# A hybrid attention and convolution layer: the low parts of the first phase's weights made on VectorE, some operands made anew, and the convolution paced by stretch

## The chip, the cores and the metric

One core of a Trainium2 chip. Its engines are TensorE (PE, with its weight loads as PEld), VectorE (DVE), ScalarE (ACT), GpSimd (POOL) and SyncE (SP, which here only issues DMAs). The metric is device time in microseconds (us) of one execution, the median of several runs. Six views of one profiled execution are used: the page, busy time by windows, groups of instructions by line, waits, one line's instructions, and the timeline.

## The reference

One layer over x of 2048 rows by 1024 channels, float32. x is normalised by row, then multiplied by `w_in` (1024 x 9216), whose columns fall into nine parts of 1024: q, k, v, a gate z for the attention, a value and a gate for the convolution, a gate z for the convolution, and two merge gates.

```python
h = x @ w_in
q, k, v, z_sb, c_val, c_gate, z_cv, g_sb, g_cv = jnp.split(h, SPLIT_POINTS, axis=-1)
o_sb = _stick_breaking_attention(to_heads(q), to_heads(k), to_heads(v)).reshape(bsz, seq, SB_WIDTH)
y_sb = (o_sb * jax.nn.silu(z_sb)) @ w_sb_proj
u = c_val * jax.nn.sigmoid(c_gate)
u = _causal_depthwise_conv(u, conv_w, conv_b)
u = jax.nn.silu(_layer_norm(u, conv_ln_g, conv_ln_b))
y_cv = (u * jax.nn.silu(z_cv)) @ w_cv_proj
merged = jax.nn.sigmoid(g_sb) * y_sb + jax.nn.sigmoid(g_cv) * y_cv
return _layer_norm(DEEPNORM_ALPHA * x + merged @ w_out, ln_g, ln_b)
```

The attention has 16 heads of 64; a weight is a sigmoid of a logit times the product of (1 - sigmoid) of the keys between. The convolution has 31 taps for each channel and is causal.

## The kernel before, in words

Every large product is made of float32r operands in two parts: a high part (a value rounded to float32r by a copy on ACT) and a low part (the value minus its high part). A product is then three matmuls: high by high, high by low, low by high. The helper `split` (L115 to L117) makes both parts, with ACT for the high and DVE for the low.

The sequence is held in four chunks of 512 rows, chunks 3 and 2 being half 1 and chunks 1 and 0 half 0. There are three stages.

**First phase** (`first_phase`, L741). It makes part of `x @ w_in` in *groups*. A group takes two blocks of 128 columns and both chunks of a half, and splits the 1024 inputs into two: a product of 2 x 2 blocks. Winograd's form of Strassen's scheme needs seven block products for it (P1 to P7) instead of eight. Each is 12 matmuls of 128 x 512 (`prod`, L906: four blocks of 128 inputs, three matmuls each), so a group is 84, in 14 pieces of six. Half 1 has 36 groups: eight u (value and gate of the convolution) and 28 of k, q, v, z, c, g and h (m = 0 to 3; g and h are the two merge gates). Half 0 has 20: eight u and twelve of c, g and h. Its k, q, v and z are made later, by the plain scheme, in the attention stage.

A group's seven weight operands come from four raw blocks: `raws` (L861) loads them, 256 KB each, on SP's queue, one group ahead. `w_op` (L869) makes one operand: for four of the seven a sum or difference on DVE first (`diff`, L877), then the high part on ACT (L891), then `low` (L901). `low` writes the negated high part into the low part's place (ACT, L902), and an accumulating DMA issued by POOL adds the raw block to it (L903). Raw blocks and differences go round in eight buffers (`raw_tile`), the operands in nine (`op_tile`). A finished operand of 512 KB is stored to device memory by SP's queue (L895, issued at L93): for k, q, v and z three of the seven, which the later stages load again; for u, c, g and h all seven, which half 0 loads instead of making them (`kept`, L873).

In a group, the seven results share PSUM banks: after P7, DVE adds its bank into the tile `gt` (L961, recorded at L757), and P4, which is issued after the next group's P1, goes on accumulating into that same bank. So P4 can't start before that addition has read it. The operands of x are made from rows that are normalised and transposed (L788, L818), and swapped for the other half's at the end of half 1 (`swap`).

**Attention stage.** The attention of half 1, then of half 0, woven with the rest of `x @ w_in`, the convolution's norm and the projections. **Output stage**: the last projections and the output product.

The convolution runs on DVE as a background job through the first two stages. A generator (`conv_steps`) makes one instruction a step: 51 steps for 128 channels and a half, 46 of them taps (L409), and two empty ones where its input wasn't loaded ahead. `slow_step` (L1115) is called after each piece of matmuls: it adds a pace to a counter and runs one step when the counter is at least 1. The pace is `PACES[phase]`: 1.0 in the first phase, 0.6 after. The counter is cut to 1 only in calls that run no step.

Order: TensorE's order is written out by hand; the other engines' instructions are put in an order by a scheduler when the kernel is built, by priority (`use` functions get 500 places of precedence, convolution steps go 800 back and at least 3 pieces late). On the chip each engine and each DMA queue runs in that order and waits at its head.

Of the kernel before, what the change touches and what calls it, by code (L numbers as in the profile page):

```python
# [8 lines left out]
F32 = mybir.dt.float32  # L9
F32R = mybir.dt.float32r  # L10
AF = mybir.ActivationFunctionType
ALU = mybir.AluOpType
# [15 lines left out]
NBW = 4  # L28
LEAD = 4.0
LAG = 3  # L30
PACES = [1.0, 0.6]
I0 = 1
SPLIT = 0.27
RD = 9
# [20 lines left out]
def layer_kernel(ctx: ExitStack, tc, x, w_in, w_sb, w_cv, w_out, vecs, cw, rows, out):  # L55
# [7 lines left out]
    nc = tc.nc  # L63
# [27 lines left out]
    def dma(dst, src):  # L91

        nc.sync.dma_start(out=dst.bitcast(F32) if dst.dtype == F32R else dst,  # L93
                          in_=src.bitcast(F32) if src.dtype == F32R else src)
# [42 lines left out]
    def st(dt=F32):  # L137
        return sg_p.tile([P, CH], dt, name="st", tag="st", bufs=7)
# [20 lines left out]
    class Fill:  # L159
# [7 lines left out]
        def add(self, cost, fn):  # L167
            self.pieces.append((cost, fn))
            for e in self.later:
                e[0] -= 1  # L170
            due = [e[1] for e in self.later if e[0] <= 0]
            self.later = [e for e in self.later if e[0] > 0]
            self.pieces += due
# [69 lines left out]
    def half(h):  # L243
        return (2 * h + 1, 2 * h)
# [32 lines left out]
    def use_qk(dr, i):  # L277
        def use(c, ps):
            hi, lo = st(F32R), st(F32R)
            split(ps, hi, lo)  # L280
            dma(dr[c, i][0], hi)
            dma(dr[c, i][1], lo)
        return use

    def v_parts(i):
        vs = {}

        def use(c, ps):
            v, vs[c] = st(), st()
            nc.scalar.activation(v, ps, AF.Copy)  # L290
            dma(vtd[c, i], v)
            n = CH - 1
            nc.vector.tensor_tensor(out=vs[c][:, :n], in0=v[:, 1:], in1=v[:, :n], op=ALU.subtract)
            if c == NCH - 1:
                nc.gpsimd.tensor_scalar(out=vs[c][:, n:], in0=v[:, n:], scalar1=-1.0, scalar2=None, op0=ALU.mult)
            else:
                nc.gpsimd.tensor_tensor(out=vs[c][:, n:], in0=vnext[:, i:i + 1], in1=v[:, n:], op=ALU.subtract)
            if c:
                nc.gpsimd.tensor_copy(out=vnext[:, i:i + 1], in_=v[:, 0:1])

        def turn(c):
            tp = tpt()
            for j in range(4):
                nc.tensor.transpose(out=tp[:, j * P:(j + 1) * P], in_=vs[c][:, j * P:(j + 1) * P], identity=ident)
            for a in range(2):
                t = st(F32R)
                tv = t.rearrange("p (b e d) -> p b e d", b=4, e=2)
                split(tp.rearrange("p (b e d) -> p b e d", b=4, e=2)[:, :, a], tv[:, :, a], tv[:, :, 1 - a])
                dma(vdr[c, i, a], tv.rearrange("p b e d -> p b (e d)"))

        return use, lambda F, c: F.delay(3, 0.44, lambda: turn(c))
# [24 lines left out]
    def gated(m, h):  # L336

        val, gate = {}, {}

        def put(c):  # L340
            if c not in val or c not in gate:
                return
            u = st()
            nc.vector.tensor_tensor(out=even_odd(u), in0=val.pop(c), in1=gate.pop(c), op=ALU.mult)
            q = c % 2 * 256
            dma(udr[h, m][:, :, q:q + 256], u.rearrange("p (e n) -> p e n", e=2))
            if c == 2 * h:
                slow.append(conv(m, h))

        def use_v(c, ps):  # L350
            val[c] = ps
            put(c)

        def use_g(c, ps):
            nc.scalar.activation(ps, ps, AF.Sigmoid)
            gate[c] = ps
            put(c)

        return use_v, use_g
# [381 lines left out]
    def first_phase(F, x2, w1, ps_p):  # L741
# [8 lines left out]
        def x_op(op, f):  # L750
            pool, tag = (x2, op) if op in ("S2", "S3", "S4") else (xa, "SX" if op == "S1" else op)
            t = [pool.tile([P, CH], F32R, name=tag + e) for e in "hl"]
            xo.setdefault(op, []).append(t)
            split(f, *t)
# [85 lines left out]
        def swap(op):  # L840

            def one(k):
                if k == 0:
                    xo[op] = []
                f = st()
                dma(f, {"A11": fdr[1][:, k], "A12": fdr[1][:, k + 4], "A22": fdr[0][:, k + 4]}[op] if op[0] == "A" else sdr[op, k])
                x_op(op, f)
            return [(0, lambda k=k: one(k)) for k in range(4)]
# [50 lines left out]
                    wdr[id(w_in), g["cols"][p == P3], int(p != P1)] = d  # L899

        def low(t, src):  # L901
            nc.scalar.activation(t[:, 1], t[:, 0].bitcast(F32), AF.Copy, scale=-1.0)  # L902
            nc.gpsimd.dma_start(out=t[:, 1], in_=src.bitcast(F32R), accum_op=ALU.add)  # L903


        def prod(g, p, part, bank, start=False):  # L906
# [68 lines left out]
        kept = {}  # L975

        def group(h, e, m):
            g = {"h": h, "after": [None, None]}
            if e == "u":
                g["cols"] = COL_CV + m * P, COL_CG + m * P  # L980
                g["uses"] = gated(m, h)
            else:
                i = 2 * m, 2 * m + 1
                base = {"k": COL_K, "q": COL_Q, "v": COL_V}.get(e) if e in "kqv" else blocks[e][0]
                g["cols"] = tuple(base + n * P for n in i)
                if e == "v":
                    g["uses"], g["after"] = zip(*(v_parts(n) for n in i))
                elif e in "kq":
                    g["uses"] = [use_qk(kdr if e == "k" else qdr, n) for n in i]
                else:  # L990
                    g["uses"] = [(silu_to if e in "zc" else sig_to)(n, blocks[e][1]) for n in i]
            if h == 0:
                g["kept"] = kept[e, m]
            else:
                g["keep"] = "some" if e in "kqvz" else "all"
                g["to"] = kept.setdefault((e, m), {})
            return g

        def order(h):
# [21 lines left out]
        for n, g in enumerate(groups):  # L1021
            nxt = groups[n + 1] if n + 1 < len(groups) else None
            last = nxt is None or nxt["h"] != g["h"]
            first = n == 0
            pc = pieces(g, nxt)
            if nxt and not first:
                F.add(0, lambda nxt=nxt: raws(nxt))

            def emit(p, extra=()):
                extra = list(extra)  # L1030
                for q in pc[p]:
                    F.add(*q)
                    if extra:
                        F.extend([extra.pop(0)])
                F.extend(extra)
                if first and p < 3:
                    for q in (4 + p,):
                        F.add(0, lambda q=q: w_op(groups[0], q))
                if last and p != P4 and nxt is not None:
                    F.extend(swap(XOP[p]))  # L1040

            emit(P1, two[:2] if first else ())
            if prev is not None:
                for q in prev[P4]:
                    F.add(*q)
                if prev_g["after"][0]:
                    prev_g["after"][0](F, half(prev_g["h"])[1])
                if prev_g["h"] != g["h"]:
                    F.extend(swap("A22"))

            def w_start():
                for p in (0, 1, 2):
                    w_next(p)

            def w_next(p):
                if nxt:
                    F.add(0, lambda nxt=nxt: w_op(nxt, p))

            if not first:
                w_start()  # L1060
            emit(P2, two[2:] if first else ())
            if g["after"][0]:
                g["after"][0](F, c1_of(g))
            if not first:
                w_next(3)
            emit(P5)
            if first:
                F.add(0, lambda nxt=nxt: raws(nxt))
                w_start()
                w_next(3)  # L1070
            w_next(4)
            emit(P6)
            w_next(5)
            emit(P3)
            if g["after"][1]:
                g["after"][1](F, c1_of(g))
            w_next(6)
            emit(P7)
            if g["after"][1]:
                g["after"][1](F, half(g["h"])[1])  # L1080
            prev, prev_g = pc, g
# [17 lines left out]
    def c1_of(g):  # L1099
        return half(g["h"])[0]  # L1100
# [3 lines left out]
    F = Fill()  # L1104
# [4 lines left out]
    phase = [0]  # L1109
# [5 lines left out]
    def slow_step(now=False):  # L1115
        marks.append(newest())
        pace[0] += PACES[phase[0]]
        if not now and (not slow or pace[0] < 1):
# [22 lines left out]
        emit_fill(len(F.pieces))  # L1141
    F = Fill()
    n_done[0] = 0
    phase[0] = 1


    with ExitStack() as s2:
# [169 lines left out]
```

## Time and profile before

| what | us |
| --- | --- |
| median of 3 runs (3349.89 to 3355.69) | 3353.22 |
| the profiled execution | 3352.82 |
| its span, first to last instruction | 3351.0 |
| TensorE matmuls busy | 2948.6 (88%) |
| VectorE busy | 2423.2 (72%) |
| ScalarE busy | 1540.5 (46%) |
| GpSimd busy | 291.8 (9%) |

Busy time counts the time in which at least one instruction of the engine runs. A window row gives, for a stretch of the span, the busy time of each engine with its number of instructions, the mean clock granted to TensorE (1.00 is full), the mean busy share of the 16 DMA engines and their GB/s. A row of groups gives a line, engine, operation, output and inputs by the program's names, shapes and count; then the busy time and the mean of one in ns; then the idle time of the engine just before, and what ended it. A row of waits gives who waited for whom, the total in us, how often, and the longest. SPq is the sequencer of SP, which issues DMAs. Matmuls overlap in their records: the distance of two starts is what one costs.

### The profile page before, as it was taken

Reading aid. Unit: us, or ns where it says so; the run is one execution under the profiler, and the core shown is the slowest. Engines: PE = TensorE matmul, PEld = TensorE weight load, DVE = VectorE, ACT = ScalarE, POOL = GpSimd, SP = SyncE. Lnnn points to the kernel's source line nnn. Section 1 sums busy time; section 2 is a strip of 40 time slices with the busy share of each in tenths; the row PEclk is TensorE's granted clock in tenths of the full one; section 3 lists DMA queues with packets and bytes.
Section 4 is the critical chain, followed back from the end, with each engine's and each line's share of the span. In section 5 each row is a group of like instructions: output and inputs, shape, how many; then the busy total and the mean of one; then the engine's idle time right before and its main releaser. Section 6 shows DMA issues by size and latency. Waiting matters only on the chain.

```text
span 3351.0 us, 42860 instructions
## 1 busy us (share of the span) xinstructions
PE 2948.6 (88%) x14666; PEld 2433.7 (73%) x14666; DVE 2423.2 (72%) x3219; ACT 1540.5 (46%) x2792; POOL 291.8 (9%) x414
## 2 busy tenths in 40 slices
PE   6676788878888999989998998999899989889998
PEld 4555666767677888778877777778778777667887
DVE  6542676554654866689899889898897888966746
ACT  7554454545453212245555455555564555543322
POOL 2222222222220000000000000000000000000000
PEclk9888888989899999999999999999999999989999
DMA  7999999999999877675656344354543544478462
GB/s 203 275 274 300 281 286 302 272 287 292 286 284 326 262 247 255 226 220 184 192 189 190 117 153 156 120 172 140 162 143 125 159 156 137 151 238 275 140 203 82
DMA packets 364203, 708.86 MB, mean 212 GB/s; under 512 B 42448, under 2 KB 84560, under 8 KB 363856
## 3 DMA queue, kind: packets, MB, share of 16 engines
q1 hardware_dynamic: 327696, 640.05, 57.3%
q0 software_dynamic: 36288, 66.08, 11.4%
q8 instruction: 115, 1.88, 0.2%
q14 instruction: 104, 0.85, 0.1%
HBM read 371.47 MB, written 268.44 MB: 191 GB/s over the span
## 4 chain that ended last, share of the span: by engine, by line
PE 36%; DVE 17%; issue 11%; DMA 6%; ACT 3%; SPq 1%; POOL 1%; DVEq 0%; POOLq 0%; ACTq 0%
PE mm L201 10%; DVE nb L589 8%; PE pb L910 6%; PE pp L910 4%; PE mm L910 4%; PE pv L628 4%; DVE tl L117 4%; PE tp L612 4%; PE lg L583 2%; PE lg L584 2%; SPq L93 1%; ACT nb L586 1%; ACT th L116 1%; DMA st<-ydq 1%; PE mo L1242 1%
## 5 line engine op out<-in xcount | busy, mean ns | idle before, releaser
L116 ACT ACTIVATE th<-tp 128x512 fp32r<-128x512 f32 (+1 forms) x576 | 330.1, 574 | 447.8 <-PE tp L612 437.1
L117 DVE TENSOR_TENSOR tl<-tp,th 128x512 fp32r<-128x512 f32 (+1 forms) x576 | 372.9, 650 | 89.8 <-ACT th L116 87.2
L612 PE MATMUL tp<-ident,nb 128*128 128x128 f32 x2176 | 352.7, 278 | 74.1 <-DVE nb L589 58.5
L586 ACT ACTIVATE nb<-lg 128x512 f32<-128x512 f32 (+3 forms) x640 | 331.1, 532 | 115.7 <-PE lg L584 113.5
L589 DVE TENSOR_TENSOR_SCAN nb<-nb,dd 128x256 f32<-128x256 f32 (+7 forms) x256 | 343.3, 1346 | 16.1 <-ACT nb L586 16.1
L628 PE MATMUL pv<-tl,v 128*128 128x256 f32 (+1 forms) x1152 | 303.2, 292 | 43.4 <-DVE tl L117 42.5
L612 PEld LDWEIGHTS tp<-ident,nb 128*128 128x128 f32 x2176 | 255.1, 142 | 108.9 <-DVE nb L589 72.0
L589 DVE TENSOR_TENSOR_SCAN nb<-nb,zero 128x1024 f32<-128x1024 f32 x128 | 299.8, 2345 | 22.3 <-ACT nb L586 22.0
L628 PE MATMUL pv<-th,v 128*128 128x256 f32 (+1 forms) x1152 | 307.8, 285 | 2.4 <-ACT th L116 2.2
L583 PE MATMUL lg<-k,qd 128*128 128x512 f32 (+3 forms) x640 | 267.6, 419 | 22.3 <-ACT nb L586 10.7
L628 PEld LDWEIGHTS pv<-tl,v 128*128 128x128 f32 x1152 | 219.0, 190 | 81.7 <-DVE tl L117 66.4
L584 PE MATMUL lg<-k,ql 128*128 128x512 f32 (+3 forms) x640 | 234.4, 366 | 0.0
L628 PEld LDWEIGHTS pv<-th,v 128*128 128x128 f32 x1152 | 219.3, 190 | 20.5 <-ACT th L116 4.6
L409 DVE SCALAR_TENSOR_TENSOR cy<-cu,csum,cy 128x512 f32<-128x512 f32 x240 | 179.3, 747 | 25.4 <-ACT cy L405 20.2
L201 PE MATMUL mm<-A11h,w 128*128 128x512 f32 x512 | 184.4, 406 | 11.6 <-ACT w L116 6.1
L201 PE MATMUL mm<-SXh,w 128*128 128x512 f32 x512 | 183.9, 405 | 1.9 <-DVE st L712 1.9
L201 PE MATMUL mm<-A12h,w 128*128 128x512 f32 x512 | 184.4, 406 | 0.0
L201 PE MATMUL mm<-A22h,w 128*128 128x512 f32 x512 | 183.5, 405 | 0.0
L409 DVE SCALAR_TENSOR_TENSOR cu<-cd,cwt,cu 128x512 f32<-128x512 f32 x240 | 178.8, 745 | 4.2
L409 DVE SCALAR_TENSOR_TENSOR cy<-cu,cwt,cy 128x512 f32<-128x512 f32 x240 | 178.7, 745 | 3.4
L583 PEld LDWEIGHTS lg<-k,qd 128*128 128x128 f32 x640 | 122.0, 191 | 47.1 <-ACT nb L586 28.4
L910 PE MATMUL pb<-A22h,w4x 128*128 128x512 f32 x256 | 99.7, 454 | 49.0 <-DVE gt L757 49.0
(253 smaller groups left out, 6551.6 us busy)
## 6 DMA issues: line engine op xcount, KB each, us to landing
wdr<-w4x SPq DMA_DIRECT2D x108, 512.0 KB, 5.4
wdr<-w SPq DMA_DIRECT2D x80, 512.0 KB, 5.1
w4x<-wdr SPq DMA_DIRECT2D x76, 512.0 KB, 4.5
w<-wdr SPq DMA_DIRECT2D x64, 512.0 KB, 4.4
w4x<-wrx POOLq DMA_DIRECT2D x100, 256.0 KB, 6.2
w<-wdr SPq DMA_DIRECT2D x96, 256.0 KB, 3.8
k<-kdr SPq DMA_DIRECT2D x192, 128.0 KB, 3.1
v<-vdr SPq DMA_DIRECT2D x96, 256.0 KB, 3.2
```

The source lines that it names most:

```text
L93: nc.sync.dma_start(out=dst.bitcast(F32) if dst.dtype == F32R else dst, in_=src.bitcast(F32) if src.dtype == F32R else src)
L116: nc.scalar.activation(hi, src, AF.Copy)
L117: nc.vector.tensor_tensor(out=lo, in0=src, in1=hi.bitcast(F32), op=ALU.subtract)
L201: nc.tensor.matmul(box["ps"], lhsT=l[:, kb], rhs=r[kb], start=(kb == 0 and n == 0), stop=(kb == KB - 1 and n == 2))
L409: nc.vector.scalar_tensor_tensor(out=dst, in0=src[:, j:j + HN], scalar=t, in1=first, op0=ALU.mult, op1=ALU.add)
L583: nc.tensor.matmul(lg[:, :w], lhsT=qd[c][:, js], rhs=k2[kc][:, ko:ko + w], start=True, stop=False)
L584: nc.tensor.matmul(lg[:, :w], lhsT=ql[c][:, js], rhs=k2[kc][:, ko:ko + w], start=False, stop=True)
L586: nc.scalar.activation(nb[:, o:o + w], lg[:, :w], AF.Sigmoid, scale=-QS)
L589: nc.vector.tensor_tensor_scan(out=nb[:, :w], data0=nb[:, :w], data1=dd[:, :w] if diag else zero.to_broadcast([P, w]), initial=0.0 if diag ...
L612: nc.tensor.transpose(out=tp[:, at_:at_ + P], in_=tiles[j][:, so:so + P], identity=ident)
L628: nc.tensor.matmul(o[:, :w], lhsT=lv, rhs=tt[:, o0:o0 + w], start=(diag and t == 0 and n == 0 and e == 0), stop=(last and t == nt - 1 and ...
L910: nc.tensor.matmul(bank, lhsT=wt[:, e, kb], rhs=xs_[kb][a], start=start and kb == 0 and n == 0, stop=kb == 3 and n == 2, skip_group_check= ...
```

## The change

Three edits go together.

1. `low` becomes one subtraction on DVE: raw block minus high part. ACT's negated copy and POOL's accumulating DMA are gone.
2. The operands of g and h with m = 0, 1 and 2 (six groups) are no longer stored in half 1; in half 0 these six groups load their raw blocks and make their operands anew. Nothing of what half 0 makes anew is stored.
3. `PACES` has three entries: 0.78 in the first phase until half 0's first group has issued its first product and half 1's last its P4, 1.25 from there to the end of the first phase, and 0.6 after.

```diff
-PACES = [1.0, 0.6]
+PACES = [0.78, 1.25, 0.6]
...
         def low(t, src):
-            nc.scalar.activation(t[:, 1], t[:, 0].bitcast(F32), AF.Copy, scale=-1.0)
-            nc.gpsimd.dma_start(out=t[:, 1], in_=src.bitcast(F32R), accum_op=ALU.add)
+            add(t[:, 1], src, t[:, 0].bitcast(F32), ALU.subtract)
...
-            if h == 0:
+            if h == 0 and (e, m) in kept:
                 g["kept"] = kept[e, m]
             else:
-                g["keep"] = "some" if e in "kqvz" else "all"
-                g["to"] = kept.setdefault((e, m), {})
+                g["keep"] = "" if h == 0 or e in "gh" and m % 4 != 3 else "some" if e in "kqvz" else "all"
+                if g["keep"] == "all":
+                    g["to"] = kept.setdefault((e, m), {})
             return g
...
                 if prev_g["h"] != g["h"]:
                     F.extend(swap("A22"))
+                    F.add(0, lambda: phase.__setitem__(0, 1))
...
-    phase[0] = 1
+    phase[0] = 2
```

## The prediction

> **What bounds the kernel now.** I read the page's DMA queues first (packets, MB, share of the 16 engines), then the busy time in three stretches, then the waits inside the first stretch, then the timeline around one stall. The stretches are the groups of the first half of the sequence (their first matmul stands at 30.47, the first of the other half at 1030.65), the twenty groups of the other half, and the rest; a row of that view has the busy time of PE, PEld, DVE, ACT and POOL, the granted clock, the DMA share and GB/s.
>
> ```profile
> q1 hardware_dynamic: 327696, 640.05, 57.3%
> q0 software_dynamic: 36288, 66.08, 11.4%
> ```
> ```profile
> 30.00:1031.00 1001.00, 795.14 (x3212) 629.63 (x3211) 552.66 (x846) 503.54 (x896) 238.38 (x305) 0.89 0.98 280
> 1031.00:1420.00 389.00, 387.58 (x1680) 314.84 (x1678) 249.56 (x349) 88.62 (x146) 0.28 (x1) 1.00 0.78 259
> 1420.00:3351.00 1931.00, 1758.04 (x9748) 1483.45 (x9748) 1600.01 (x1977) 930.00 (x1722) 40.02 (x81) 0.98 0.52 165
> ```
> ```profile
> 30.47 0.77 PE L910 MATMUL mm<-A11h,w 128*128 128x512 f32 x1
> ...
> 1030.65 0.39 PE L910 MATMUL mm<-A11h,w 128*128 128x512 f32 x1
> ...
> 1399.90 0.40 PE L910 MATMUL mm<-A11h,w4x 128*128 128x512 f32 x1
> ```
>
> The two halves issue the same 84 matmuls a group. The first takes (1030.65 - 30.47) / 36 = 27.8 us a group, the other (1399.90 - 1030.65) / 19 = 19.4. The other half is bound by TensorE (387.6 busy of 389, clock 1.00). In the first half no engine is full: TensorE 0.79, DVE 0.55, ACT 0.50; only the 16 DMA engines are (0.98). So 8.4 us a group are lost to something that only the first half does, and it makes its weight operands there. The waits of that stretch say how (us in total, times, longest):
>
> ```profile
> SPq L93 <- DMA w4x<-wrx: 130.9, 47, 24.2
> SPq L93 <- DMA w<-wrx: 95.0, 34, 7.8
> SPq L93 <- DMA w4x<-wraw: 65.8, 25, 6.6
> SPq L93 <- DMA w<-wraw: 61.8, 25, 6.4
> ```
> ```profile
> DVE wrx L757 <- DMA wrx<-in_w_in: 119.5, 27, 12.7
> DVE wrx L757 <- DMA w<-wrx: 61.9, 17, 15.1
> DVE bs L255 <- DMA mu<-in_x: 32.0, 5, 12.7
> DVE wrx L757 <- DMA w4x<-wrx: 27.5, 9, 7.7
> ...
> DVE st L757 <- DMA st<-fdr: 20.8, 2, 16.5
> ```
> ```profile
> PE pb L910 <- DVE gt L757: 85.3, 24, 8.9
> ```
>
> SP's queue stands 353.5 us before stores of finished operands (L93), waiting for the accumulating DMAs of L903; the loads of the next raw blocks (L867) are queued behind. DVE, in order too, then stands in a difference (L879) for a raw block or for a buffer that an accumulating DMA still reads: 119.5 + 61.9 + 27.5 = 209 us. Behind that stands the addition of L961, and product P4 goes on accumulating into the bank that it reads, so TensorE waits there: 85.3 us, in two groups of three. Each such stall costs a second time:
>
> ```profile
> 622.38 0.50 PE L910 MATMUL pb<-A22h,w4x 128*128 128x512 f32 x1 [2.49 <-DVE gt L757]
> ...
> 623.85 1.05 PE L910 MATMUL pb<-A22h,w4x 128*128 128x512 f32 x2
> ...
> 627.28 0.62 PE L910 MATMUL mm<-A12h,w4x 128*128 128x512 f32 x2
> ```
>
> After 2.49 us of idling, pairs of matmuls take 1.05 instead of 0.62 us for some 3.4 us, which loses 1.7 us more; the mean clock of the stretch is 0.89.
>
> **The change part by part.** (1) *What the low parts cost now.* Seven operands in each of 36 groups are 252 (ns: least, median, most; then first and last start in us):
>
> ```profile
> L902 ACT ACTIVATE w4x<-w4x x140: 612/632/637, 50.2 to 996.7; 128x512 fp32r<-128x512 f32 x140
> L902 ACT ACTIVATE w<-w x112: 612/632/671, 15.4 to 986.1; 128x512 fp32r<-128x512 f32 x112
> ```
>
> ACT loses 252 x 0.632 = 159 us. I cost this gain at nothing: ACT is at 0.50, and what it makes late for TensorE is small. POOL loses 252 issues; nothing in the first phase hangs on POOL but small work. The DMA engines lose all of queue q0: 66.08 MB is 252 x 256 KB, and 11.4% of 3351 is 382 us of the 16 engines, out of 0.98 x 1001 = 981.
>
> (2) *What they cost after.* One subtraction each. The same form stands in a later stage, and two neighbours show the pitch of such instructions back to back:
>
> ```profile
> L117 DVE TENSOR_TENSOR w<-wraw,w 128x512 fp32r<-128x512 f32 x80 | 53.8, 683 | 14.4 <-ACT w L116 11.9 <-PE tp L612 1.3 <-PE lg L584 1.0
> ```
> ```profile
> 727.97 0.68 DVE L757 TENSOR_TENSOR wrx<-wrx 128x512 f32<-128x512 f32 x1
> 728.57 0.68 DVE L757 TENSOR_TENSOR gt<-pb,gt 128x512 f32<-128x512 f32 x1
> ```
>
> So 252 x 0.60 to 0.683 = 151 to 172 us more on DVE; I take 162. The subtraction adds a wait for ACT's copy of the high part, with the additions before P4 and the convolution queued behind it; the row's idle time is 14.4 / 80 = 0.18 us each, 45 us in all, which is in the idle share of step 5.
>
> (3) *Six groups made anew* (g and h of m = 0, 1, 2). The first half stores 42 operands of 512 KB less: 22 MB, at 57.3% x 3351 / 640 = 3.0 us a MB that is 66 us of the 16 engines, and 42 fewer waiting stores in SP's queue. In the other half 42 loads of 512 KB in SP's queue become 24 raw loads of 256 KB; ACT gets 42 copies, DVE 24 differences (0.68) and 42 subtractions, 45 us at 0.68. ACT is at 0.23 there and hides its part.
>
> (4) *Pace.* One call of the pacer runs at most one convolution step, whatever the pace, and what is not used is kept. So 1.25 gives one step a call in the other half, as 1.0 did, and the surplus is drawn down after. Counting calls (14 a group) and the 51 steps of a convolution gives 380 steps before the other half instead of 431, 276 instead of 263 in it, and 160 instead of 148 after, at first one a call instead of 0.6. Their time:
>
> ```profile
> 30.00:1031.00 1001.00, 272.18 (x368) 0.89 0.98 280
> 1031.00:1420.00 389.00, 176.56 (x238) 1.00 0.78 259
> 1420.00:3351.00 1931.00, 96.28 (x131) 0.98 0.52 165
> ```
>
> (these are the taps of L409 in the three stretches). 50 of a convolution's steps occupy DVE, mostly with taps of 0.74 us. So 51 steps are 35 us less in the first half, and 13 and 12 steps some 9 us more in each of the others.
>
> (5) *The first half, summed.* DMA: 981 - 382 - 66 = 533 us of transfers, so they bound nothing above that; at 781 us their share would be 0.68, and the other half runs full at 0.78. TensorE's floor: 36 x 19.4 = 698, and the transposes, which the other half lacks:
>
> ```profile
> L304 PE MATMUL tp<-ident,st 128*128 128x128 f32 x64 | 12.3, 318 | 38.6 <-DVE st L293 34.5 <-ACT st L822 3.9
> L788 PE MATMUL tp<-ident,xr 128*128 128x128 f32 x68 | 11.4, 306 | 7.8 <-ACT st L791 7.8
> ```
> ```profile
> 1017.40 0.79 PE L910 MATMUL pp<-S4h,w4x 128*128 128x512 f32 x1 [4.85 <-ACT gt L945]
> ```
>
> 23.7 us, 12 more for the 64 of the later rows (L818, as many as L304's), and 5 for a wait in the swap of the operands at the end, which the change leaves in place: 739. DVE: 552.7 + 162 - 35 = 680. An in-order engine with such waits isn't full; how full it gets where it paces a stage is seen in the attention:
>
> ```profile
> 1450.00:2450.00 1000.00, 894.06 (x1080) 0.99 0.52 164
> 1800.00:1850.00 50.00, 48.26 (x63) 1.00 0.62 196
> ```
>
> At 0.965 (the best 50 us) the 680 take 705, less than TensorE's floor, which then decides; at 0.83 (the mean after 1420) 819; at 0.894 they take 761. I take the last, since that stage too runs both engines near their limit, and add 20 of the 53 us that DVE stands for loads of x and fdr, which the change leaves in place. So 781 instead of 1000: **-219**, with 739 and 839 (819 + 20) as ends. DVE is what is late next, in place of the DMA engines.
>
> (6) *The other half.* DVE goes from 249.6 to 249.6 + 45 + 9 = 304 of 389, but in the three pairs of remade groups it has about 7.5 + 10.4 + 1.4 = 19.3 us of work (seven subtractions and four differences, 14 steps, two additions) in 19.4. Nothing if the slack of the neighbours absorbs it; at most a stall of 2.5 + 1.7 us in each of six groups, 25. I take **+6**.
>
> (7) *The attention.* 9 us more of taps, and denser at its start. Nothing where TensorE paces; 9 / 0.894 = 10 where DVE does, and as much again if the denser start isn't paid back. I take **+8**.
>
> The profiled execution took 3352.8 us, 1.8 beside its span and 0.4 under the median. 3352.8 - 219 + 6 + 8 = **3148 us**.
>
> **The weight of one rule.** The cost of a short stall decides how bad a busy DVE gets. The row above has 2.49 us of idling followed by 3.4 us at half rate. The Trainium skill (TensorE: Matmul & The Clock Gate, HAM oscillation) states that gaps of more than about 3.4 us are what drops the clock; by it a stall of 2.5 us would cost itself alone, and rival B below would come to 739 + 36 x 2.5 = 829 us and 3196 instead of 3257. The trace disagrees, so I go by the row.
>
> **The rivals.**
>
> A. *DVE hides everything*; the first half runs at TensorE's floor of 739, and steps 6 and 7 cost nothing: 3352.8 - 261 = 3092. For it: DVE's 680 are under 739. Against it: that is 0.92 for a whole stage, which only short stretches show.
>
> B. *The addition before P4 stays late*, now behind subtractions instead of DMAs, in every group: 2.5 us of stall and 1.7 of slow clock on the floor, 739 + 36 x 4.2 = 890, so 3352.8 - 110 + 14 = 3257. For it: this stall is there in two groups of three with DVE at 0.55. Against it: the rows give its cause as loads and buffers held by DMAs, and the addition is issued ahead of the convolution.
>
> C. *Slower: DVE's idle time isn't the DMAs' doing.* In the first half DVE idles 1001 - 553 = 448 us. If the raw loads stay as late, since they are issued one group ahead and SP's stores now wait for DVE itself, that idle time stays, and the stage is 680 + 448 = 1128: 3352.8 + 128 + 14 = 3495. It turns slower from 306 us of idle time on (1000 - 680 - 14). Against it: 209 of the 448 stand before differences, for DMAs that go or are relieved; the other half shows no such waits.
>
> D. *No change*, the gain eaten by the later stretches: it would need 200 us there, and nothing shows them.
>
> **How the numbers follow.** Forecast 0.55 (3108 to 3206, by the ends of step 5), A 0.18, B 0.20, C 0.05, D 0.02. A measurement here tells 0.2%, 6.7 us, from nothing. Faster 0.93, same 0.02, slower 0.05. The range holds the forecast, A and most of B: 3085 to 3270.
>
> **What would show it.** Queue q0 gone and the DMA share of the first half near 0.7 (step 1, 3); the first half's groups at about 21.7 us each and the other half starting near 812 instead of 1031; DVE near 680 us busy there, with the clock above 0.95 (step 5); SP's waits for accumulating DMAs gone, its stores waiting for DVE; some 395 us for the other half (step 6); about 140 taps after it, done earlier (steps 4, 7). Stalls before P4 in nearly every group would mean B; the differences still standing for raw loads by over 100 us, C. The forecast is wrong if DVE's share in the first half stays under 0.8, or if the taps that moved slow the attention by more than 20 us.

## The result, and the profile after

| | median us | ratio to the kernel before (95%) |
| --- | --- | --- |
| before, on the same chip | 3351.55 | |
| changed | 3144.98 | 0.9385 (0.9365 to 0.9405) |
| forecast | 3148 (3085 to 3270) | |

The total is 3 us from the forecast, and the profiled execution (3146.5 us, span 3144.7) 206 us shorter than the one before. The gain lies where it was put, but that the total came so close is in part luck: the sum holds two errors that cancel. I cut both traces at four places of TensorE's timeline: the first matmul of group 1, of group 37 (the other half's first), the first logits of the attention, the last matmul of its value products.

| stage, us | before | changed | difference | forecast |
| --- | --- | --- | --- | --- |
| start | 30.5 | 27.1 | -3.4 | 0 |
| first half, 36 groups | 1000.2 | 772.6 | -227.6 | -219 |
| other half, 20 groups, and the switch | 403.1 | 404.3 | +1.2 | +6 |
| attention | 1515.3 | 1537.2 | +21.9 | +8 |
| from there to the end | 402.0 | 403.4 | +1.4 | 0 |

Of the page of the changed kernel, the slices and the DMA queues:

```profile
PE   6998999999999998899889889998899888879998
...
PEclk8999999999999999999999999999999999989999
...
q1 hardware_dynamic: 319056, 602.29, 58.3%
```

Queue q0 is gone, and with it 66 MB. The busy time by windows (PE, PEld, DVE, ACT, POOL, granted clock, DMA share, GB/s): the first half, its steady part, the other half, the attention.

```profile
27.00:800.00 773.00, 737.34 (x3210) 594.69 (x3210) 678.09 (x1077) 357.20 (x649) 30.36 (x61) 0.98 0.71 250
...
380.00:775.00 395.00, 391.56 (x1712) 318.23 (x1712) 352.63 (x546) 167.27 (x293) 8.96 (x20) 1.00 0.68 241
...
800.00:1190.00 390.00, 387.55 (x1681) 315.16 (x1680) 297.45 (x431) 111.86 (x188) 0.82 (x2) 1.00 0.66 215
```
```profile
1204.00:2741.00 1537.00, 1387.65 (x8154) 1182.84 (x8155) 1348.46 (x1590) 798.58 (x1542) 16.62 (x27) 0.98 0.50 156
```

And the attention of the kernel before:

```profile
1434.00:2949.00 1515.00, 1382.58 (x8155) 1179.66 (x8156) 1339.58 (x1580) 799.14 (x1541) 19.34 (x27) 0.98 0.50 158
```

DVE works 678.1 us in the first half, where 680 was forecast, and the DMA engines stand at 0.71, where 0.68 was. But from 380 us on it is TensorE that is full: 391.6 of 395 us at clock 1.00, with DVE at 0.89. The waits of the first half (who, for whom, us in total, times, longest) show the same.

```profile
PE pb L909 <- ACT st L950: 10.1, 3, 5.6
PE tp L304 <- DVE st L293: 6.6, 4, 1.9
PE tp L788 <- ACT st L791: 5.9, 5, 2.8
PE pb L909 <- DVE gt L757: 4.5, 2, 3.9
```
```profile
DVE w L757 <- ACT w L891: 17.2, 24, 2.1
DVE w4x L757 <- ACT w4x L891: 10.7, 18, 1.4
...
DVE wrx L757 <- DMA wrx<-in_w_in: 5.4, 7, 1.7
```
```profile
SPq L93 <- DVE w4x L757: 119.5, 60, 24.2
SPq L93 <- DVE w L757: 73.1, 56, 4.6
```

The stall of P4 behind the addition is 4.5 us instead of 85.3, and the differences stand 5.4 us for raw blocks instead of 119.5. SP's stores now wait for the subtractions, 192.6 us, where they waited 353.5 us for accumulating DMAs. The subtractions themselves (L902, recorded at L757) take what the row of the same form said, 0.683:

```profile
L757 DVE TENSOR_TENSOR w4x<-wrx,w4x 128x512 fp32r<-128x512 f32 x100 | 68.6, 687 | 11.5 <-ACT w4x L891 10.1 <-DMA wrx<-in_w_in 0.7
L757 DVE TENSOR_TENSOR w<-wrx,w 128x512 fp32r<-128x512 f32 x78 | 53.6, 688 | 19.2 <-ACT w L891 17.2 <-DMA ydr<-cu 1.6
```

### The profile page after: what moved, and what is told of

The parts are those of the page before. It is cut to its first block, busy times and chain, and to the rows that moved or that the text cites. A ratio compares the mean times of both kernels' runs of the same rounds, so it can differ in the third digit from the quotient of the medians.

```text
span 3144.7 us, 42164 instructions
## 1 busy us (share of the span) xinstructions
PE 2896.8 (92%) x14666; PEld 2402.7 (76%) x14666; DVE 2603.8 (83%) x3537; ACT 1414.0 (45%) x2582; POOL 75.4 (2%) x162
## 4 chain that ended last, share of the span: by engine, by line
PE 47%; DVE 25%; issue 12%; DMA 7%; ACT 3%; SPq 1%; POOL 1%; DVEq 0%; POOLq 0%; ACTq 0%
PE pb L909 11%; PE mm L201 10%; DVE nb L589 10%; PE pp L909 7%; PE mm L909 7%; DVE tl L117 4%; PE tp L612 4%; PE pv L628 3%; PE lg L583 1%; DVE cy L409 1%; PE lg L584 1%; ACT th L116 1%; DVE cu L409 1%; ACT nb L586 1%; DMA st<-fdr 1%
## 5 line engine op out<-in xcount | busy, mean ns | idle before, releaser
L612 PE MATMUL tp<-ident,nb 128*128 128x128 f32 x2176 | 354.6, 279 | 80.4 <-DVE nb L589 63.5
L612 PEld LDWEIGHTS tp<-ident,nb 128*128 128x128 f32 x2176 | 255.2, 142 | 116.7 <-DVE nb L589 78.8
L584 PEld LDWEIGHTS lg<-k,ql 128*128 128x128 f32 x640 | 123.7, 193 | 8.8 <-issue 0.2
```

The costliest lines, as they stand in the source:

```text
L584: nc.tensor.matmul(lg[:, :w], lhsT=ql[c][:, js], rhs=k2[kc][:, ko:ko + w], start=False, stop=True)
L612: nc.tensor.transpose(out=tp[:, at_:at_ + P], in_=tiles[j][:, so:so + P], identity=ident)
```

## The experiments

Two things were open: whether the bound that fell was the room on the DMA engines or the chain of waits for each accumulating DMA; and why the attention lost 22 us. Times in the column of medians are of four to six executions; ratios are to the kernel before on the same chip, with 95% intervals. Stage times come from one profiled execution of each run, and the executions of one kernel differ by 4 to 23 us here, so a few us in one stage of one run show little; what several runs share counts.

| run | first half | other half | attention | median | ratio |
| --- | --- | --- | --- | --- | --- |
| before | 1000 | 403 | 1515 | 3351.6 | 1 |
| changed | 773 | 404 | 1537 | 3145.0 | 0.9385 (0.9365 to 0.9405) |
| low parts alone | 782 | 405 | 1518 | 3134.2 | 0.9354 (0.9334 to 0.9375) |
| all stored | 782 | 408 | 1544 | 3154.8 | 0.9421 (0.9399 to 0.9442) |
| no surplus | 770 | 407 | 1530 | 3135.0 | 0.9364 (0.9343 to 0.9385) |
| spare DMAs | 941 | 412 | 1541 | 3321.7 | 0.9913 (0.9882 to 0.9944) |
| two a call | 774 | 405 | 1515 | 3122.9 | 0.9309 (0.9294 to 0.9324) |
| old pace | 773 | 405 | 1522 | 3129.3 | 0.9320 (0.9298 to 0.9341) |
| two a call from 1.0 | 776 | 405 | 1508 | 3123.9 | 0.9310 (0.9293 to 0.9327) |
| two a call, all stored | 782 | 408 | 1508 | 3127.1 | 0.9317 (0.9292 to 0.9341) |
| anew alone | 970 | 420 | 1518 | 3335.3 | 0.9943 (0.9925 to 0.9962) |
| low parts on GpSimd | 850 | 425 | 1538 | 3252.0 | 0.9704 (0.9669 to 0.9738) |
| pace 1.5 | 778 | 409 | 1511 | 3127.7 | 0.9326 (0.9300 to 0.9352) |

### The low parts alone

The kernel before with one edit.

```diff
-            nc.scalar.activation(t[:, 1], t[:, 0].bitcast(F32), AF.Copy, scale=-1.0)
-            nc.gpsimd.dma_start(out=t[:, 1], in_=src.bitcast(F32R), accum_op=ALU.add)
+            add(t[:, 1], src, t[:, 0].bitcast(F32), ALU.subtract)
```

> Only the low parts move to VectorE; all operands are still stored, and the paces are 1.0 and 0.6 as before. Theory 1 (the accumulating DMAs alone held the first half, TensorE's floor of about 19.4 us a group is what is left, and the attention of the changed kernel lost 23 us to convolution steps that came denser): VectorE has 552.7 + 160 = 713 us of work in the first half, which takes some 785 us against 773 in the changed kernel; the other half 389; the attention and the rest 1917 from its first logits on, as before. Total about 3135, 10 us under the changed kernel. Theory 2 (all three edits are needed: with 1.0 step a call VectorE paces the first half at 0.88 of its time): the first half takes 713 / 0.88 = 812 and more, total 3160 or over.

Measured 3134.2, a first half of 782 and an attention of 1518. Theory 1 holds: the first edit alone brings all of the gain, and the other two together, as they were made, give 11 us of it back by the medians (0.9354 against 0.9385; the intervals overlap, so this alone doesn't show it).

### All operands stored

```diff
-                g["keep"] = "" if h == 0 or e in "gh" and m % 4 != 3 else "some" if e in "kqvz" else "all"
+                g["keep"] = "" if h == 0 else "some" if e in "kqvz" else "all"
```

> The changed kernel with all operands stored in the first half and loaded in the other, none made anew. Theory 1 (with the accumulating DMAs gone the DMA engines have room): their share in the first half goes from 0.71 to about 0.78 and nothing else moves; total within 6 us of the changed kernel, 3139 to 3151. Theory 2 (stores waiting in SP's queue are what is left of the old chain, 192 us of waits): 42 more of them make the first half 15 us or more longer, total 3160 or over.

Measured 3154.8, 10 us over the changed kernel and between the two theories. The first half is 782 instead of 773. The three runs with all operands stored (this one, the low parts alone, and one below) have 782; where six groups are made anew and the low parts are made on VectorE, without spare DMAs, it is 770 to 778. So the 42 stores cost some 9 us there although the DMA engines have room (0.77). A forecast of mine, that the stores had no price once the DMA engines had room, is wrong by that. The 9 us lie in the first 14 groups (342 us instead of 334), which hold only g and h of m = 0, so 14 of the 42 stores; the later groups take the same time with and without the other 28. What it is in those groups that the stores delay isn't shown. Nothing follows here on the pace: this run at 0.78 and the low parts alone at 1.0 both have 322 taps in the first half.

### No surplus

```diff
-PACES = [0.78, 1.25, 0.6]
+PACES = [0.78, 1.0, 0.6]
```

> The changed kernel with a pace of 1.0 instead of 1.25 in the other half. The number of steps in the two halves is the same by the pacer's code; only the surplus of about 69 steps that 1.25 leaves is gone, so the 140 taps after the other half are spread as before, 0.6 a call. Theory 1 (the denser steps at its start slow the attention): the stretch after the first logits takes 1917 to 1928 instead of 1941, total 3122 to 3134. Theory 2 (the attention lost its 23 us to the nine more taps, or to something else): total 3140 to 3150.

Measured 3135.0, a us over the upper end of theory 1, and 1932 us from the first logits on, where 1917 to 1928 was expected. The number of taps in the three stretches is the same as in the changed kernel, 338, 260 and 138, as the reading of the pacer had it; only their density after the other half changes. The attention goes from 1537 to 1530. The first 600 us of the attention show what dense taps do: the changed kernel, then this one.

```profile
1204.00:1804.00 600.00, 540.68 (x3149) 461.06 (x3150) 544.33 (x691) 292.75 (x590) 10.98 (x16) 0.97 0.55 170
1804.00:2741.00 937.00, 846.97 (x5007) 721.78 (x5006) 804.13 (x900) 505.84 (x953) 5.64 (x11) 0.99 0.47 147
```
```profile
1203.00:1803.00 600.00, 554.60 (x3268) 474.81 (x3269) 526.36 (x655) 305.08 (x614) 10.49 (x16) 0.98 0.56 172
1803.00:2734.00 931.00, 838.27 (x4891) 713.13 (x4890) 822.09 (x937) 495.16 (x930) 7.03 (x11) 0.97 0.46 147
```

With all its taps in the first 600 us, DVE is at 0.91 instead of 0.88 and TensorE gets 3149 instead of 3268 matmuls done. The rest, without taps, makes up only part of that.

Seven us between two executions would be little to go by, but more runs show the same. The first third of the attention, counted by the transposes of L612 (725 of 2176, in TensorE's fixed order), is here for the changed kernel, this one and the one before:

```profile
1204.00:1757.80 553.80, 500.15 (x2905) 426.65 (x2905) 501.16 (x639) 269.95 (x547) 9.08 (x13) 0.97 0.55 169
1203.30:1735.80 532.50, 493.90 (x2906) 423.04 (x2907) 465.43 (x583) 269.47 (x546) 8.60 (x13) 0.98 0.57 174
1433.80:1955.30 521.50, 487.86 (x2905) 419.13 (x2905) 464.80 (x584) 268.61 (x545) 10.39 (x13) 0.99 0.56 176
```

It takes 553 to 555 us in the four runs with the surplus (changed, all stored, spare DMAs, low parts on GpSimd), with 128 taps in it; and 522 to 532 in the five that have 129 to 138 taps after the other half and spread them at 0.6 a call (before, low parts alone, anew alone, no surplus, old pace), with 75 to 78 in it. The other two thirds take 983 to 989 and 991 to 998. So 50 taps more cost some 28 us on average where they come densely, and their absence later gives back some 9. Why this run, with its taps spread, is still 8 to 15 us longer in the attention than the others with spread taps isn't settled; it has nine taps more.

### Spare DMAs

The changed kernel, and beside each subtraction an accumulating DMA of 256 KB whose result nothing uses.

```diff
             add(t[:, 1], src, t[:, 0].bitcast(F32), ALU.subtract)
+            n = count["d"]
+            count["d"] += 1
+            if n < 8:
+                spare.append(dram([P, 4, P], F32R, f"spare{n}"))
+                dma(spare[n], t[:, 0])
+            nc.gpsimd.dma_start(out=spare[n % 8], in_=t[:, 0], accum_op=ALU.add)
```

> The changed kernel, and beside each subtraction an accumulating DMA of the same 256 KB from the operand's high part into a spare tensor in device memory, which no instruction of the computation waits for; the output isn't touched. Theory 1 (the room on the 16 DMA engines was the bound): 533 us of transfers in the first half and 380 of such DMAs are 913 us and more, so the first half takes 920 to 1000 instead of 773, total 3290 to 3370. Theory 2 (the chain of waits for each accumulating DMA was the bound, and the full DMA engines only its picture): the first half stays within 30 us, total under 3180.

Measured 3321.7, with a first half of 941 us, its queues and its waits:

```profile
q0 software_dynamic: 42336, 77.09, 14.3%
```
```profile
25.00:966.00 941.00, 775.65 (x3210) 617.31 (x3209) 680.01 (x1080) 354.85 (x651) 245.84 (x312) 0.92 0.99 279
```
```profile
DVE wrx L758 <- DMA wrx<-in_w_in: 99.4, 25, 9.8
```
```profile
PE pb L916 <- DVE gt L758: 74.3, 18, 10.1
```

Theory 1 holds. The instructions of the computation hardly wait for these transfers (they read an operand, so its buffer can't be written again before; the view of waits puts 5.3 us of DVE's idle time down to that), and yet the old picture comes back: DMA engines at 0.99, differences that stand for raw blocks (99.4 us), P4 behind the addition (74.3 us), a clock of 0.92. 168 of the 228 us are taken back by load on the DMA engines. DVE's work is the same as without them (680 us against 678).

### The six groups made anew, alone

The kernel before with the edits of `group` (L992 to L996) and nothing else; accumulating DMAs and paces stay.

> The kernel before with the six groups made anew and nothing else: accumulating DMAs and old paces stay. Theory 1 (the room on the 16 DMA engines is the bound of the first half): 42 stores of 512 KB less are 66 us of transfers, and the first half takes 925 to 945 instead of 1000; in the other half the DMA engines trade 66 us of loads for 83 us of raw loads and accumulating DMAs and stay under 0.85, so 404 to 420; total 3280 to 3300. Theory 2 (the chain of waits for each accumulating DMA is the bound): the first half stays above 980, total 3330 and over.

Measured 3335.3 and a first half of 970, which is neither theory's figure.

```profile
30.00:1001.00 971.00, 786.72 (x3212) 623.83 (x3211) 553.77 (x847) 502.25 (x894) 240.75 (x305) 0.91 0.95 266
```

The DMA engines are relieved of 0.98 x 1001 - 0.95 x 971 = 59 us of transfers, close to the 66 worked out, but the stage shortens by 30. Most of the waits stay (79.8 us before P4 against 85.3), so at a share of 0.95 the waits of the chain seem to count too. How the last 60 us of the first half's gain divide between the stores and the chain isn't settled by these runs.

### The old pace

```diff
-PACES = [0.78, 1.25, 0.6]
+PACES = [1.0, 1.0, 0.6]
```

> The changed kernel (low parts on VectorE, six groups made anew) with the old paces 1.0, 1.0 and 0.6. Theory 1 (VectorE isn't what paces the first half; the 42 stores cost it 9 us): first half 773, the other 404, 1919 from the first logits on, total 3122 to 3130, under both the changed kernel and the one with the low parts alone. Theory 2 (VectorE paces the first half): 0.22 x 490 steps of 0.72 us more there make it 20 us or more longer, total 3140 and over.

Measured 3129.3. Theory 1 holds at every stage: 773, 405 and 1522. The windows of the first half and of the attention:

```profile
27.00:800.00 773.00, 735.07 (x3208) 591.61 (x3208) 694.31 (x1105) 354.86 (x647) 36.20 (x61) 0.98 0.71 250
...
1205.00:2727.00 1522.00, 1387.89 (x8157) 1184.25 (x8157) 1340.46 (x1580) 799.52 (x1542) 19.31 (x27) 0.98 0.49 157
```

DVE does 28 more taps in the first half (366 against 338, 16 us more busy) and the half takes as long. The pace of 0.78 relieves an engine that doesn't set the end there, and pushes its work to a stage where it does harm. The edit of the paces costs 16 us (0.9385 against 0.9320, intervals apart).

### Two steps a call

The changed kernel with a pacer that spends what its counter holds, so that 1.25 is 1.25.

```diff
-        pace[0] -= 1
-        with tc.high_priority(offset=-800), tc.issue_after(marks[max(0, len(marks) - 1 - LAG)]):
-            while slow and next(slow[0], slow) is slow:
-                slow.pop(0)
+        while True:
+            pace[0] -= 1
+            with tc.high_priority(offset=-800), tc.issue_after(marks[max(0, len(marks) - 1 - LAG)]):
+                while slow and next(slow[0], slow) is slow:
+                    slow.pop(0)
+            if now or not slow or pace[0] < 1:
+                break
```

> The changed kernel with a pacer that runs as many steps as the counter holds, so that 1.25 is really 1.25 steps a call in the other half and leaves no surplus. By the pacer's code 91 steps stay for the attention instead of 160. Theory 1 (in the attention VectorE decides, and each step that it is spared is worth its 0.72 us or more): the stretch from the first logits on goes from 1941 to about 1895 (1880 to 1910), the other half stays at 404, total 3090 to 3115. Theory 2 (the attention is held by its own chain of engines, and steps fill gaps): it stays above 1917, total 3122 and over. Theory 3 (VectorE, at 0.88 of the other half, makes TensorE wait there): the other half is longer by 15 us or more.

Measured 3122.9, outside the 3090 to 3115 of theory 1 and within theory 2's total (3122 and over), with 1913 us from the first logits on. The other half takes 61 more taps (321 against 260) at no cost:

```profile
801.00:1190.00 389.00, 387.59 (x1680) 314.83 (x1679) 342.96 (x496) 113.09 (x190) 0.00 (x0) 1.00 0.67 219
1206.00:2721.00 1515.00, 1383.62 (x8152) 1183.09 (x8153) 1306.44 (x1523) 797.56 (x1540) 17.08 (x27) 0.98 0.49 157
```

DVE is at 0.88 of the other half and TensorE at 1.00, so theory 3 falls. The attention is 22 us shorter with 61 taps (42 us of DVE's busy time) less. Against the run with the old pace it is 7 us shorter with 52 taps less (129 to 77): when taps come 0.6 a call, most of them lie in gaps, as theory 2 had it. What costs is density, as the first thirds above show.

### Two steps a call, paces from 1.0

The same pacer with [1.0, 1.25, 0.6], with the six groups made anew, then with all stored.

> Made anew as in the changed kernel, a pacer that runs as many steps as the counter holds, and paces 1.0, 1.25 and 0.6: 82 steps stay for the attention. Theory 1: first half 773, the other 404 to 410, about 1885 from the first logits on, total 3085 to 3110, the best of these. Theory 2 (the attention held by its own chain): 3120 and over. Theory 3 (VectorE full in the other half): the other half over 420.

> As the run before, but with all operands stored and none made anew, which leaves VectorE 45 us less work in the other half and costs 42 stores in the first. Theory 1: first half 782, the other 404, about 1885 from the first logits on, total 3093 to 3120, some 9 us over the run with six groups made anew. Theory 3 (VectorE full in the other half where six groups are made anew): this one is the faster of the two.

Measured 3123.9 and 3127.1: in the first half and the other half about as theory 1 had it (776 and 405; 782 and 408), but the attention falls to 1508 only, with 69 taps left (1909 us from the first logits on, where 1885 was expected). So the total of the first is in theory 2's 3120 and over. Stored or made anew differ by 6 us in the first half, and not clearly in the median (3 us, the intervals overlap).

### Pace 1.5

The first of these two with [1.0, 1.5, 0.6].

> Six groups made anew, a pacer that runs as many steps as the counter holds, and paces 1.0, 1.5 and 0.6: 25 steps stay for the attention instead of 82. VectorE in the other half comes to about 385 of 390 us. Theory 1 (VectorE full makes TensorE wait for the additions before P4): the other half over 420 instead of 405, and the attention about 1500, total 3120 to 3140. Theory 2 (convolution steps simply come later than planned and fill gaps): the other half at 405 to 410, total 3110 to 3122.

Measured 3127.7, within the total of theory 1 but not for its reason: the other half stays under its 420. VectorE came to 338 us of 391 and not to 385, so the case of a full VectorE wasn't reached. The other half is 409 us, 4 more than at 1.25; and the attention, with 46 taps left, takes 1511, no less than with 69. This pace brought nothing more.

```profile
804.00:1195.00 391.00, 388.74 (x1678) 315.75 (x1677) 338.20 (x492) 112.86 (x189) 0.00 (x0) 1.00 0.66 218
```

### The low parts on GpSimd

```diff
-            add(t[:, 1], src, t[:, 0].bitcast(F32), ALU.subtract)
+            nc.gpsimd.tensor_tensor(out=t[:, 1], in0=src, in1=t[:, 0].bitcast(F32), op=ALU.subtract)
```

> The changed kernel with the subtraction of the low parts on GpSimd instead of VectorE; paces 0.78, 1.25, 0.6 as in it. Theory 1 (neither engine paces the first half, TensorE's floor does): if GpSimd takes less than 2.7 us for a subtraction (seven a group of 19.4 us), the first half stays at 773 within 15, total 3130 to 3155, with VectorE near 520 us busy there. Theory 2 (VectorE paced it): the first half falls to 745 or less, total under 3120. Theory 3 (GpSimd too slow, or the two engines slow each other): first half over 800.

Measured 3252.0 with a first half of 850 us: theory 3, and of its two readings the rows show the second (those of the taps and the subtractions are of 30 to 800 us). GpSimd has time (395 us of 850), but DVE, relieved of 36 x 7 subtractions, is busy for longer than with them:

```profile
29.00:879.00 850.00, 757.27 (x3209) 603.48 (x3209) 704.34 (x830) 354.32 (x649) 395.47 (x309) 0.96 0.65 227
```
```profile
L409 DVE SCALAR_TENSOR_TENSOR cy<-cu,csum,cy 128x512 f32<-128x512 f32 x105 | 112.4, 1071 | 3.0 <-ACT cy L405 1.3
```
```profile
L902 POOL TENSOR_TENSOR w4x<-wrx,w4x 128x512 fp32r<-128x512 f32 x92 | 133.7, 1454 | 120.9 <-ACT w4x L891 108.8 <-DVE cu L409 2.8 <-DMA wrx<-in_w_in 2.7
```
```profile
PE pb L909 <- DVE gt L757: 42.6, 20, 6.0
```

A tap takes 1.07 us on average instead of 0.75, and P4 waits again (42.6 us). How much of the 77 us comes from that, and how much from a subtraction that is ready later than VectorE's would be, isn't separated: DVE also stands 23 us in the differences for buffers that GpSimd still reads. Of one line's instructions, least, median and most ns show which kind is slowed: a difference of two SBUF tiles, and an addition that reads one operand from PSUM.

```profile
L757 DVE TENSOR_TENSOR wrx<-wrx x84: 675/687/1792, 14.6 to 1148.3; 128x512 f32<-128x512 f32 x84
L757 DVE TENSOR_TENSOR st<-pp,st x56: 675/683/692, 71.1 to 1285.3; 128x512 f32<-128x512 f32 x56
```

## Why the prediction was right, point by point

*What bounds the kernel (right).* The DMA engines held the first half: with the transfers put back and hardly any instruction waiting for them, it is at 941 again, of 1000 before. The chain that the prediction read from the waits (SP's stores, raw blocks, differences, the addition, P4) is how that shortage reached TensorE, and appears again in the run with spare DMAs although its first link is gone.

*Steps 1 and 2 (right in kind; one number by luck).* 0.687 us a subtraction against 0.683; DMA share 0.71 against 0.68. DVE's 678 us against 680 hide two errors that cancel. With the old pace, and as many taps as in the kernel before (366 and 367), it is 694.3, so the 252 subtractions add 142 us to the 552.7 and not 162, 0.56 each, below the step's own lower bound of 151. And the pace of 0.78 saves 694.3 - 678.1 = 16 us and not 35.

*Step 3 (sizes off).* The stores that went were counted as 66 us of transfers behind a stage with room, so at nothing; they are worth 9 us in the first half (773 against 782), all of it in the first 14 groups. Making the operands anew was put at +6 in the other half, which took 1 us more than before: there was slack enough.

*Step 4 (right in the reading, not in the price).* 1.25 gives no more steps than 1.0 in the other half: 260 taps with either. The counts of 380, 276 and 160 steps came out as 338, 260 and 138 taps. The step's own counts don't match in their sums (842 steps before, 816 after). Of taps, whose sum stays the same, 29 left the first half, and 20 and 9 came to the two others.

*Step 5 (right in its time, 781 against 773; wrong in its reason).* "DVE is what is late next, in place of the DMA engines" is the sentence that fell. In the groups from 380 us on, TensorE runs at its floor of 19.4 us with DVE at 0.89, and 16 us more on DVE move nothing (the old pace). That is rival A's mechanism. Most of the 34 us that the half lies above the floor of 739 are in its first 13 groups: 310 us for a floor of 13 x 19.4 = 252 and most of the transposes. In these TensorE waited 19.5 us for ScalarE and 7.2 for VectorE, and the mean clock was 0.95; what sets their time wasn't tested. The share of 0.894, taken from the attention, put about as much time into the sum as those first groups lose, and that was chance. (The lower end of the forecast's own range, 3108, is 3106 by the step's numbers.)

*Step 7 (the term that was mis-sized).* +8 was taken and +22 measured, over the step's upper end of 20, and over the 20 us that the prediction's last sentence named as a sign that it is wrong. The same 138 taps cost 7 us less when they come at 0.6 a call, and 129 taps at 0.6 give 1522 or less. The prediction named the denser start, and took it for work that is paid back later in most of the sum. It mostly isn't: the first third of the attention took 32 us more than before, and the rest 10 less.

So -230 before the attention against -213, and +23 from there on against +8: 17 us better and 15 us worse than forecast.

*The rivals.* B and C didn't come: 4.5 us of waiting before P4, 5.4 us for raw blocks. Since P4 hardly stalled, the weight of the rule on the clock gate wasn't put to the test by the total. Single gaps of the changed kernel go the way of the prediction's row, though not each time: after 1.89 us of idling at 344.91, pairs of matmuls took 1.05 us again; after 1.64 us at 524.47 they took 0.63.

## What to carry to other kernels

When the DMA engines are full, the waits in a trace name the transfer that comes last, not the one that is too many: count the share of the engines by queue first, and take away the traffic. Relieving VectorE was worth nothing in groups where it had slack beside the bound, even at 0.89, and the work that was pushed out has to be priced where it lands, by how densely it comes there. A pacer's counter that can't be spent is a debt: two steps a call, with the same paces, made the fastest versions here (3122.9 to 3127.7, against 3145.0 for the change as it was made), though the old pace alone comes to 3129.3, and the intervals don't tell these apart.

## What the runs showed of the hardware that was not expected

GpSimd and VectorE slowed each other. With the subtractions on GpSimd (1.45 us on average in the row above, 1.25 at the least), DVE's instructions that read two tiles of SBUF were stretched: taps to 1.07 us on average instead of 0.75, differences to as much as 1.79 where their median is 0.687. The additions that read one operand from PSUM kept their time (0.692 at the most in the row above). Two copies of a single SBUF tile (L430) were stretched as well, to 1.51 and 1.40 us from 0.42. The Trainium skill (SBUF — State Buffer, SBUF: two separate sides) says that a GpSimd instruction that reads SBUF and a VectorE instruction with two SBUF inputs, or in a mode with two ports, take an exclusive lock on a shared pair of ports, and that the loser waits for the whole instruction. This trace agrees for the instructions with two SBUF inputs: they are slowed, and the most that a difference of the row above loses, 1.79 - 0.69 = 1.1 us, is less than the shortest GpSimd subtraction. Whether the two copies ran in such a mode no run shows.

DVE was 0.89 busy over 395 us, in order, and TensorE waited for it 3.4 us in that time. A high share of an in-order engine was not by itself a sign that it was late.
